# A hybrid decoder layer on one core: the gate products of its linear attention as one float32r pass, and its decays computed within the state space part

## The chip, the core and the metric

One NeuronCore of a Trainium2 chip runs the whole layer as one program. The metric is the device time of one execution in microseconds (us), smaller is better; times given are medians over several executions.

## What is computed

One layer over 512 tokens of width 1024, everything in float32. Cut to what matters here:

```python
h = rms_norm(x, mixer_norm)
q, k, v, g_out, a_lr, z, xbc, dt_raw, gate_a, gate_b = split_cols(h @ w_in, ...)
# linear attention: 4 heads, key width 128 a head, value width 256 a head, chunks of 64
g_log = log_sigmoid(a_lr @ w_gate + b_gate) / 16     # a_lr: 512 x 16, w_gate: 16 x 512
b     = cumsum(g_log within each chunk)
q_t   = q * 128**-0.5 * exp(b);  k_t = k * exp(-b)
o     = causal(q_t k_t^T) v + q_t S_prev             # and k * exp(b_last - b) builds the next state
o_a   = rms(o) * head_norm * silu(g_out)
o_b   = ssd_mixer(z, xbc, dt_raw, ...)               # state space part, 4 groups, chunks of 128
x     = x + (sigmoid(gate_a) * (o_a @ w_branch_a) + sigmoid(gate_b) * (o_b @ w_branch_b)) @ w_out
...                                                  # conv-gated MLP, gated embedding, final norm
```

The change concerns `a_lr @ w_gate` and what is made of it up to `b`.

## The kernel before, in words

**Products.** A float32 product is nearly everywhere made of three float32r passes: each operand is split into a float32r part (`whi`, `h1h`: a cast on ScalarE, L161) and the rest (`wlo`, `h1l`: a subtraction on VectorE, L162), and TensorE multiplies high by high, high by low and low by high into one PSUM tile (`mm3`, L165 to L168). `proj_a` (L170) computes output columns on the partitions, one PSUM tile `pa` of 128x512 for each 128 columns, 24 passes when the inner width is 1024. `proj_b` (L221) computes tokens on the partitions, four PSUM tiles `pb` at once. Both take their tiles from four PSUM banks (tag `mm`, L79); the cores, the transposes and the gate products share four others (tag `sm`, L82). A bank is free again when the function `emit` of the projection has read it.

**Order of the work.** First the norm and its transposes; then the step-size stage (L671 to L734), in which one projection `psdt` of 48 columns gives `dt_raw` and `a_lr`; then the state space part (L736 to L753), for each group `g` a projection (`ssd_proj`), a preparation (`ssd_pre`), the core (`ssd_core`, L584), the gate projection (`ssd_z`), the branch product of the group before (`ssd_branch`) and the gating (`ssd_gate`); then the linear attention (L757 to L927): decays, and for each pair of heads three projections (`gla_pair_proj`, L793: v, then q and k, then g) and two cores (`gla_core`, L846); then the merge (L930 to L968): four pairs of sigmoid gates (`gate_pair`) and four pairs of branch columns (`branch_pair`); then w_out, the MLP and the rest. The order on each engine is not written by hand: a planner takes the instructions that are ready by priority. The priority falls with the place in the program; weight loads and splits are lifted by 100000 (`ahead`, L133), `emit` by 50000, the step-size chain by 60000, and the last `ssd_branch` is put back by 1200 (L750). The order is then fixed, and each engine works through its own queue in it, the DMA queues of SyncE (SP) and ScalarE (ACT) among them.

**The gate products and the decays before.** `alr` (16x512, on partitions 32 to 47) and `wgt` are float32; `wgt` is loaded by one DMA right after the parameters (L492), `alr` is copied out of `psdt` by ScalarE (L677). After the state space part, L770 to L785 compute for each of the four heads: the product `gg` of 16 rows (L772) in float32, an addition, a minimum and an absolute value on VectorE (L776 to L778), Exp on ScalarE (L779), Ln (L783), a subtraction (L784) and a scan (L785) into `bcum`. `gla_pair_proj` makes three exponentials E1, E2, E3 of each `bcum` (L802 to L805), with which `emit` multiplies the projections of q and k (L813, L817, L818).

**Memory.** Pools are laid on a stack in the order in which they are opened, on the left or on the right side, and a closed pool's bytes are given to the next one. A tile of a later pool waits for the older tiles that lay in its bytes. The linear attention lies on the left as `oap` (`oah`, `oal`: 32 KB on each partition), `bcp` (four tiles of 2 KB, tag `bc`: the `bcum`, later gate outputs), then `gp` (`gsm` 2 KB, `v` 16, E1, E2, E3 4 each, `sg` 8, `att`, `qi`, `ks`, `kst` 2 each, `on` 4, `gS` 2, in this order). When `gp` is closed (L926), `mtp` (`mth`, `mtl` 16 KB each, four gate outputs of 2 KB) takes its place. `gate_pair` (L935) writes its sigmoids into `bcp` for columns 0, 1, 4, 5 and into `mtp` for 2, 3, 6, 7 (L938). On the right lies `dts` (L488), closed at L927; the residual tiles `x2` (L972) take its place and are loaded from ScalarE's queue (L974).

Of the kernel before, what the change touches and what calls it, by code (L numbers as in the profile page):

```python
# [8 lines left out]
F32 = mybir.dt.float32  # L9
# [29 lines left out]
def f32(ap):  # L39
    return ap.bitcast(F32)  # L40
# [3 lines left out]
def tile_hybrid_block(  # L44
# [120 lines left out]
    def mm3(ps, lh, ll, rh, rl, first, last):  # L165
        TE.matmul(ps, lhsT=lh, rhs=rh, start=first, stop=False)  # L166
        TE.matmul(ps, lhsT=lh, rhs=rl, start=False, stop=False)  # L167
        TE.matmul(ps, lhsT=ll, rhs=rh, start=False, stop=last)  # L168
# [318 lines left out]
    dx = ExitStack()  # L487
    dts = dx.enter_context(tc.tile_pool(name="dts", bufs=1, side="right"))  # L488

    alr = dts.tile([48, T], F32, name="alr")  # L490
    wgt = dts.tile([48, 512], F32, name="wgt")
    nc.sync.dma_start(wgt[32:48, :], w_gla_gate)  # L492
    qt = dts.tile([P, NT, P], F32, name="qt")

    dram = ctx.enter_context(tc.tile_pool(name="dram", bufs=1, space=bass.MemoryType.DRAM))
# [175 lines left out]
    if True:  # L671
        raw = wload([w_in[:, OFF_DT : OFF_DT + 32], w_in[:, OFF_ALR : OFF_ALR + 16]], KD, 48)
        dhi, dlo = wsplit(raw, KD, 48)
        ps = mm_ps("psdt")
        for k in range(KD):
            mm3(ps[:48, :], dhi[:, k, :], dlo[:, k, :], hT[0][:, k, :], hT[1][:, k, :], k == 0, k == KD - 1)
        S.copy(alr[32:48, :], ps[32:48, :])  # L677
        go = ahead(60000)
        go.__enter__()

        def tl(tag, name, rows=32):
            return sp.tile([rows, T], F32, tag=tag, name=name, bufs=2)

        xr, ab = tl("xdt", "dt_x"), tl("xdt", "dt_ab")
        s1, s2 = tl("xdc", "dt_s1"), tl("xdc", "dt_s2")
        qq, Q = tl("yt", "dt_q"), tl("yt", "dt_Q", P)
        smask = tl("S", "smask")
        G.memset(smask, 1.0)
        G.memset(smask.rearrange("p (c l) -> p c l", c=NT)[:, :, 0:1], 0.0)
        ae = cp.tile([32, 1], F32, name="ae")  # L690
        S.activation(ae, alog, AF.Exp)
        V.tensor_scalar(out=xr, in0=ps[:32, :], scalar1=dtb, scalar2=None, op0=ALU.add)
        V.scalar_tensor_tensor(out=ab, in0=xr, scalar=-1.0, in1=xr, op0=ALU.mult, op1=ALU.max)
        S.activation(ab, ab, AF.Exp, scale=-1.0)

        V.tensor_scalar(out=s1, in0=ab, scalar1=2.0, scalar2=None, op0=ALU.add)
        V.reciprocal(s1, s1)
        V.tensor_tensor(s1, ab, s1, op=ALU.mult)
        V.tensor_tensor(s2, s1, s1, op=ALU.mult)
        V.tensor_scalar(out=qq, in0=s2, scalar1=1.0 / 15.0, scalar2=None, op0=ALU.mult)  # L700
        for k in range(6, 0, -1):
            V.scalar_tensor_tensor(
                out=qq, in0=qq, scalar=1.0 / (2 * k + 1), in1=s2, op0=ALU.add, op1=ALU.mult
            )
        V.scalar_tensor_tensor(out=qq, in0=qq, scalar=1.0, in1=s1, op0=ALU.add, op1=ALU.mult)
        V.tensor_scalar(out=xr, in0=xr, scalar1=0.0, scalar2=None, op0=ALU.max)
        V.scalar_tensor_tensor(out=xr, in0=qq, scalar=2.0, in1=xr, op0=ALU.mult, op1=ALU.add)
        S.copy(Q[0:32, :], xr)

        V.tensor_scalar(out=s1, in0=xr, scalar1=ae, scalar2=None, op0=ALU.mult)  # L710
        V.tensor_tensor_scan(out=s2, data0=smask, data1=s1, initial=0.0, op0=ALU.mult, op1=ALU.add)
        S.copy(Q[32:64, :], s2)
        for c in range(NT):
            nc.scalar.dma_start(ncsd[c], s2[:, c * P : (c + 1) * P])
        S.activation(Q[64:96, :], s2, AF.Exp, scale=-1.0)
        s2v = s2.rearrange("p (c l) -> p c l", c=NT)
        V.tensor_tensor(
            s1.rearrange("p (c l) -> p c l", c=NT), s2v, s2v[:, :, P - 1 : P].to_broadcast([32, NT, P]),
            op=ALU.subtract,
        )  # L720
        S.activation(s1, s1, AF.Exp)
        V.tensor_tensor(qq, s1, xr, op=ALU.mult)
        S.copy(Q[96:128, :], qq)
        ps = sm_ps("psq")
        for c in range(NT):
            TE.transpose(ps[:, c * P : (c + 1) * P], Q[:, c * P : (c + 1) * P], ident)
        V.tensor_copy(qt, ps.rearrange("p (c q) -> p c q", c=NT))
        ps = sm_ps("pscd")
        TE.matmul(
            ps[:, : NT * 32], lhsT=ident[:, P - 1 : P].to_broadcast([P, P]), rhs=qt[:, :, 64:96],  # L730
            start=True, stop=True,
        )
        V.tensor_copy(cdb, ps[:, : NT * 32].rearrange("p (c h) -> p c h", c=NT))
        go.__exit__()  # L734

    ssd_pre(0)  # L736
    ssd_proj(0, 4, 6)
    for g in range(SG):
        ssd_core(g)
        ssd_z(g)  # L740
        if g > 0:
            ssd_branch(g - 1)
        if g + 1 < SG:
            ssd_tiles(g + 1)
            ssd_proj(g + 1, 0, 4)
        ssd_gate(g)
        if g + 1 < SG:
            ssd_pre(g + 1)
            ssd_proj(g + 1, 4, 6)
# [8 lines left out]
    oap = gx.enter_context(tc.tile_pool(name="oap", bufs=1, reuse_waits="tile"))  # L758
    oah = oap.tile([P, KD, T], R, name="oah")
    oal = oap.tile([P, KD, T], R, name="oal")  # L760
    bcp = gx.enter_context(tc.tile_pool(name="bcp", bufs=1, reuse_waits="tile"))
    ggx = ExitStack()
    gp = ggx.enter_context(tc.tile_pool(name="gp", bufs=1, reuse_waits="tile"))
    gsm = gp.tile([P, T], F32, name="gsm")
    G.memset(gsm, 1.0)
    G.memset(gsm.rearrange("p (c l) -> p c l", c=8)[:, :, 0:1], 0.0)
    bcum = [bcp.tile([P, T], F32, tag="bc", name=f"bcum{h}", bufs=4) for h in range(GH)]
    v0 = gp.tile([P, NT, 512], F32, tag="v", name="v0", bufs=2)
    gtmp = []
    for h in range(GH):  # L770
        ps = sm_ps(f"gg{h}")
        TE.matmul(ps, lhsT=wgt[32:48, h * P : (h + 1) * P], rhs=alr[32:48, :], start=True, stop=True)  # L772
        bc = bcum[h]
        e = gp.tile([P, T], F32, tag=f"E{1 + h // 2}", name=f"ge{h}", bufs=2)
        bcol = bga[:, h : h + 1]
        V.tensor_scalar(out=e, in0=ps, scalar1=bcol, scalar2=None, op0=ALU.add)  # L776
        V.tensor_scalar(out=bc, in0=e, scalar1=0.0, scalar2=None, op0=ALU.min)
        V.scalar_tensor_tensor(out=e, in0=e, scalar=-1.0, in1=e, op0=ALU.mult, op1=ALU.max)  # L778
        S.activation(e, e, AF.Exp, scale=-1.0)  # L779
        gtmp.append(e)  # L780
    for h in range(GH):
        bc, e = bcum[h], gtmp[h]
        S.activation(e, e, AF.Ln, bias=1.0)  # L783
        V.tensor_tensor(e, bc, e, op=ALU.subtract)  # L784
        V.tensor_tensor_scan(out=bc, data0=gsm, data1=e, initial=0.0, op0=ALU.mult, op1=ALU.add)  # L785

    def c64(ap):
        return ap.rearrange("p (c l) -> p c l", c=8)
# [139 lines left out]


    mtp = gx.enter_context(tc.tile_pool(name="mtp", bufs=1, reuse_waits="tile"))  # L930
    mth = mtp.tile([P, KD, T], R, name="mth")
    mtl = mtp.tile([P, KD, T], R, name="mtl")
    gates = {}
# [272 lines left out]
```

## Time and profile before

| | us |
|---|---|
| median of 3 runs | 1167.65 |
| lowest and highest | 1167.58, 1169.05 |
| the profiled execution, its time | 1167.36 |
| its span in the profile | 1165.3 |
| TensorE busy in the span | 1143.2 |

The profiled execution is one run of the program; its span goes from the first to the last instruction, and some 2 us of its time lie around it. Engines are named PE (TensorE), PEld (its weight loads), DVE (VectorE), ACT (ScalarE), POOL (GpSimd), SP (SyncE); a name with a q (SPq, ACTq) is the engine's own queue, where DMAs are issued. "L772" is a line of the kernel, `gg<-alr,wgt` an output and its inputs by the program's names. A wait is put down to the instruction whose end released it. Tokens such as "x8" count instructions.

### The profile page before, as it was taken

To read this page: it belongs to the slowest core of one execution; us is meant where nothing else is said; L and a number is where in the kernel's file an instruction comes from. 1 tells how busy PE (TensorE), PEld (TensorE's weight loads), DVE (VectorE), ACT (ScalarE), POOL (GpSimd) and SP (SyncE) were. 2 spreads that over 40 slices of the span, in tenths; PEclk is the share of its full clock that TensorE was granted. 3 is DMA by queue.
4 is the path that set the end of the run, shared out by engine and by line. 5 is a ranking of instruction groups with operands and counts; after the bars stand their busy time and mean duration, and the time that the engine had idled before them with its cause. 6 is when DMAs were issued, how large, how long until landed. Compare 5 with 4: busy or idle time off the path is not lost.

```text
span 1165.3 us, 13943 instructions
## 1 busy us (share of the span) xinstructions
PE 1143.2 (98%) x5476; PEld 947.1 (81%) x5476; DVE 698.4 (60%) x914; ACT 529.8 (45%) x850; POOL 143.4 (12%) x127
## 2 busy tenths in 40 slices
PE   6999999999999999999999999999999999999997
PEld 5888887888888777888888888898888888888786
DVE  6779687866676446343234334555665765776865
ACT  4567756755532147442433232353433433444653
POOL 4003130040041000000021110000030001201112
PEclk9999999999999999999999999999999999999999
DMA  7362443325222423224223431933517552544221
GB/s 211 109 171 70 124 113 104 109 73 145 73 73 73 145 73 109 73 73 109 73 73 91 109 100 46 244 100 109 131 50 181 143 147 73 127 136 109 92 89 73
DMA packets 152673, 125.85 MB, mean 108 GB/s; under 512 B 5776, under 2 KB 125328, under 8 KB 152608
## 3 DMA queue, kind: packets, MB, share of 16 engines
q1 hardware_dynamic: 148352, 115.98, 34.4%
q0 software_dynamic: 2912, 5.77, 2.9%
q10 hardware_dynamic: 1344, 3.21, 0.8%
q8 instruction: 43, 0.70, 0.3%
q14 instruction: 22, 0.18, 0.0%
HBM read 122.79 MB, written 2.16 MB: 107 GB/s over the span
## 4 chain that ended last, share of the span: by engine, by line
PE 92%; DVE 2%; ACT 2%; DMA 1%; SPq 1%; issue 1%; POOL 0%; POOLq 0%; ACTq 0%; DVEq 0%
PE pa L167 17%; PE pa L168 17%; PE pa L166 17%; PE pb L246 7%; PE pb L248 7%; PE pb L247 7%; PE yd L600 2%; PE sX L345 2%; PE sX L346 2%; PE sX L347 2%; DMA raw<-in_w_in_dram 1%; PE st L608 1%; PE yo L597 1%; PE sZ L347 1%; PE sZ L345 1%; PE sZ L346 1%
## 5 line engine op out<-in xcount | busy, mean ns | idle before, releaser
L162 DVE TENSOR_TENSOR wlo<-raw,whi 128x1024 fp32r<-128x1024 f32 (+1 forms) x208 | 259.7, 1256 | 200.7 <-ACT whi L161 200.4
L161 ACT CAST whi<-raw 128x1024 fp32r<-128x1024 f32 (+1 forms) x209 | 215.3, 1033 | 344.0 <-PE pa L167 230.3
L166 PE MATMUL pa<-h1h,whi 128*128 128x512 f32 (+1 forms) x416 | 158.8, 382 | 0.4 <-ACT h1h L416 0.4
L167 PE MATMUL pa<-h1l,whi 128*128 128x512 f32 (+1 forms) x416 | 157.7, 379 | 0.1
L168 PE MATMUL pa<-h1h,wlo 128*128 128x512 f32 (+1 forms) x416 | 157.1, 378 | 0.0
L167 PE MATMUL pa<-h2l,whi 128*128 128x512 f32 (+1 forms) x384 | 142.5, 372 | 0.0
L166 PE MATMUL pa<-h2h,whi 128*128 128x512 f32 (+1 forms) x384 | 142.3, 372 | 0.0
L168 PE MATMUL pa<-h2h,wlo 128*128 128x512 f32 (+1 forms) x384 | 142.0, 372 | 0.0
L246 PE MATMUL pb<-whi,h1h 128*128 128x512 f32 x256 | 100.1, 396 | 2.2 <-DVE accb L660 0.8
L247 PE MATMUL pb<-wlo,h1h 128*128 128x512 f32 x256 | 100.8, 394 | 0.0
L248 PE MATMUL pb<-whi,h1l 128*128 128x512 f32 x256 | 100.0, 393 | 0.0
L167 PEld LDWEIGHTS pa<-h1l,whi 128*128 128x128 f32 x416 | 79.2, 190 | 14.9 <-issue 1.0
L166 PEld LDWEIGHTS pa<-h1h,whi 128*128 128x128 f32 x416 | 79.3, 191 | 14.4 <-ACT h1h L416 0.8
L168 PEld LDWEIGHTS pa<-h1h,wlo 128*128 128x128 f32 x416 | 79.1, 190 | 14.3 <-issue 0.7
L168 PEld LDWEIGHTS pa<-h2h,wlo 128*128 128x128 f32 x384 | 72.3, 188 | 12.6
L167 PEld LDWEIGHTS pa<-h2l,whi 128*128 128x128 f32 x384 | 72.3, 188 | 12.4
L166 PEld LDWEIGHTS pa<-h2h,whi 128*128 128x128 f32 x384 | 72.1, 188 | 12.3
L246 PEld LDWEIGHTS pb<-whi,h1h 128*128 128x128 f32 x256 | 48.1, 188 | 13.6 <-DVE accb L660 1.2
L248 PEld LDWEIGHTS pb<-whi,h1l 128*128 128x128 f32 x256 | 48.1, 188 | 10.6 <-issue 0.7
L247 PEld LDWEIGHTS pb<-wlo,h1h 128*128 128x128 f32 x256 | 48.1, 188 | 10.6 <-issue 0.7
L528 DVE SCALAR_TENSOR_TENSOR acc<-pa,prm,acc 128x511 f32<-128x511 f32 (+2 forms) x72 | 52.7, 743 | 3.2 <-ACT acc L526 2.2
L167 PE MATMUL pa<-obl,whi 128*128 128x512 f32 x128 | 51.2, 400 | 0.0
(365 smaller groups left out, 1970.9 us busy)
## 6 DMA issues: line engine op xcount, KB each, us to landing
raw<-in_w_in_dram SPq DMA_DIRECT2D x48, 512.0 KB, 5.2
raw<-in_w_ffn_up_dram SPq DMA_DIRECT2D x44, 512.0 KB, 5.3
raw<-in_w_in_dram SPq DMA_DIRECT2D x16, 1024.0 KB, 5.1
raw<-in_w_ffn_down_dram SPq DMA_DIRECT2D x10, 1024.0 KB, 5.2
L<-ncsd SPq DMA_DIRECT2D x16, 512.0 KB, 4.6
raw<-in_w_branch_b_dram SPq DMA_DIRECT2D x32, 256.0 KB, 4.0
raw<-in_w_branch_a_dram SPq DMA_DIRECT2D x8, 512.0 KB, 4.6
raw<-in_w_out_dram SPq DMA_DIRECT2D x4, 1024.0 KB, 5.3
```

Source lines behind the costliest of these rows:

```text
L161: S.copy(hi, raw)
L162: eng.tensor_tensor(lo, raw, f32(hi), op=ALU.subtract)
L166: TE.matmul(ps, lhsT=lh, rhs=rh, start=first, stop=False)
L167: TE.matmul(ps, lhsT=lh, rhs=rl, start=False, stop=False)
L168: TE.matmul(ps, lhsT=ll, rhs=rh, start=False, stop=last)
L246: TE.matmul(pss[t], lhsT=a, rhs=hi[:, kk, :], start=first, stop=False)
L247: TE.matmul(pss[t], lhsT=a, rhs=lo[:, kk, :], start=False, stop=False)
L248: TE.matmul(pss[t], lhsT=b, rhs=hi[:, kk, :], start=False, stop=last)
L345: TE.matmul(ps, lhsT=a_h, rhs=hi[:, k % 2, :], start=new and k == 0, stop=False, skip_group_check=True)
L346: TE.matmul(ps, lhsT=a_h, rhs=lo[:, k % 2, :], start=False, stop=False, skip_group_check=True)
L347: TE.matmul(ps, lhsT=a_l, rhs=hi[:, k % 2, :], start=False, stop=k == kh - 1, skip_group_check=True)
L528: V.scalar_tensor_tensor(out=acc[:, s:], in0=ps[:, : T - s], scalar=cw[:, ct, 3 - s : 4 - s], in1=acc[:, s:], op0=ALU.mult, op1=ALU.add,)
```

## The change

`alr` and `wgt` become float32r tiles of 96 partitions. Rows 32 to 47 of `alr` hold the high part of a_lr, rows 0 to 15 its rest, rows 64 to 79 the high part again, all other rows zero; `wgt` holds the high part of the weights in rows 0 to 15 and 32 to 47 and their rest in rows 64 to 79. One pass over 96 rows then adds low by high, high by high and high by low. The weights come by three DMAs into a scratch tile of tag `L`, after GpSimd has zeroed it. The decays are computed in the state space part, after the core of its group 1, with scratch tiles of the tags `xdc`, `xdt` and `yt`; `bcum` moves into `dts`. `bcp` holds gate outputs only, and is opened after `mtp`.

```diff
-    alr = dts.tile([48, T], F32, name="alr")
-    wgt = dts.tile([48, 512], F32, name="wgt")
-    nc.sync.dma_start(wgt[32:48, :], w_gla_gate)
+    alr = dts.tile([96, T], R, name="alr")
+    wgt = dts.tile([96, 512], R, name="wgt")
+    bcum = [dts.tile([P, T], F32, name=f"bcum{h}") for h in range(GH)]
     qt = dts.tile([P, NT, P], F32, name="qt")
...
             mm3(ps[:48, :], dhi[:, k, :], dlo[:, k, :], hT[0][:, k, :], hT[1][:, k, :], k == 0, k == KD - 1)
+        wraw = sp.tile([96, 512], F32, tag="L", name="wraw", bufs=4)
+        G.memset(wraw, 0.0)
+        G.tensor_copy(alr, wraw)
+        for r in (0, 32, 64):
+            nc.sync.dma_start(wraw[r : r + 16, :], w_gla_gate)
+        S.copy(wgt, wraw)
+        V.tensor_tensor(wgt[64:80, :], wraw[64:80, :], f32(wgt[64:80, :]), op=ALU.subtract)
         S.copy(alr[32:48, :], ps[32:48, :])
+        V.tensor_tensor(alr[0:16, :], ps[32:48, :], f32(alr[32:48, :]), op=ALU.subtract)
+        S.copy(alr[64:80, :], alr[32:48, :])
         go = ahead(60000)
...
+    def gla_decays():
+        gsm = sp.tile([P, T], F32, tag="xdc", name="gsm", bufs=2)
+        G.memset(gsm, 1.0)
+        G.memset(gsm.rearrange("p (c l) -> p c l", c=8)[:, :, 0:1], 0.0)
+        gtmp = []
+        for h in range(GH):
+            ps = sm_ps(f"gg{h}")
+            TE.matmul(ps, lhsT=wgt[:, h * P : (h + 1) * P], rhs=alr, start=True, stop=True)
+            bc = bcum[h]
+            e = sp.tile([P, T], F32, tag="xdt" if h < 2 else "yt", name=f"ge{h}", bufs=2)
...
     for g in range(SG):
         ssd_core(g)
+        if g == 1:
+            gla_decays()
         ssd_z(g)
...
-    bcp = gx.enter_context(tc.tile_pool(name="bcp", bufs=1, reuse_waits="tile"))
     ggx = ExitStack()
     gp = ggx.enter_context(tc.tile_pool(name="gp", bufs=1, reuse_waits="tile"))
-    gsm = gp.tile([P, T], F32, name="gsm")
...
-    bcum = [bcp.tile([P, T], F32, tag="bc", name=f"bcum{h}", bufs=4) for h in range(GH)]
     v0 = gp.tile([P, NT, 512], F32, tag="v", name="v0", bufs=2)
...
     mtp = gx.enter_context(tc.tile_pool(name="mtp", bufs=1, reuse_waits="tile"))
+    bcp = gx.enter_context(tc.tile_pool(name="bcp", bufs=1, reuse_waits="tile"))
```

The rest of `gla_decays` is the removed L775 to L785, word for word.

## Rows read from the trace of the kernel before

**Rows 1.** The page: each engine's busy time, share of the span, instructions.
```profile
PE 1143.2 (98%) x5476; PEld 947.1 (81%) x5476; DVE 698.4 (60%) x914; ACT 529.8 (45%) x850; POOL 143.4 (12%) x127
```

**Rows 2.** Stretches: length, then PE, PEld, DVE, ACT, POOL busy, clock, DMA share, GB/s.
```profile
45.00:60.00 15.00, 15.00 (x71) 11.65 (x70) 14.08 (x17) 7.98 (x11) 0.00 (x0) 1.00 0.40 120
...
100.00:160.00 60.00, 60.00 (x309) 49.38 (x309) 48.09 (x59) 42.56 (x80) 13.11 (x11) 1.00 0.39 116
160.00:375.00 215.00, 215.00 (x1056) 176.15 (x1055) 153.16 (x182) 105.21 (x188) 44.38 (x35) 1.00 0.32 95
...
420.00:457.00 37.00, 35.55 (x155) 28.67 (x155) 27.02 (x40) 30.30 (x37) 0.00 (x0) 1.00 0.31 92
457.00:612.00 155.00, 155.00 (x734) 128.01 (x733) 55.06 (x79) 59.22 (x107) 11.46 (x18) 1.00 0.32 87
```

**Rows 3.** Waits of TensorE: waiter, releaser, us in total, times, longest.
```profile
PE pb L246 <- DVE accb L660: 0.8, 1, 0.8
PE pb L246 <- DVE E L818: 0.8, 1, 0.8
PE pb L246 <- DVE E L813: 0.7, 1, 0.7
```

**Rows 4.** Timeline of TensorE around one gate product: start, duration, engine, line.
```profile
382.61 0.39 PE L167 MATMUL pa<-obl,whi 128*128 128x512 f32 x1
...
384.42 0.39 PE L166 MATMUL pa<-obh,whi 128*128 128x512 f32 x1
384.74 1.12 PE L772 MATMUL gg<-alr,wgt 16*128 16x512 f32 x2
385.79 0.50 PE L167 MATMUL pa<-obl,whi 128*128 128x512 f32 x1
386.12 0.40 PE L168 MATMUL pa<-obh,wlo 128*128 128x512 f32 x1
```

**Rows 5.** Instructions on `ge` alone, 419 to 457 us: length, DVE busy, ACT busy.
```profile
419.00:457.00 38.00, 14.21 (x20) 5.06 (x8) 1.00 0.30 90
```

**Rows 6.** ScalarE's groups, 380 to 460 us: busy, mean ns, idle before.
```profile
L783 ACT ACT_TABLE_LOAD x4 | 5.1, 1283 | 0.1
```

**Rows 7.** Step-size stage: instructions on `dt_Q` (ns, start), SyncE's load of `wgt`.
```profile
L726 PE MATMUL psq<-ident,dt_Q x4: 270/272/272, 81.4 to 81.7; 128*128 128x128 f32 x4
...
L723 ACT COPY dt_Q<-dt_q x1: 618/618/618, 78.2 to 78.2; 32x512 f32<-32x512 f32 x1
...
14.38 0.43 SPq L492 DMA_DIRECT2D wgt<-in_w_gla_gate_dram  x1
```

**Rows 8.** ScalarE's queue: two of the four loads of `x2`.
```profile
390.01 0.82 ACTq L974 DMA_DIRECT2D x<-in_x_dram  x2
```

**Rows 9.** Instructions on `pa` alone, by stretch: TensorE's passes first.
```profile
556.60:587.00 30.40, 21.29 (x87) 16.10 (x87) 0.00 (x0) 1.77 (x3) 1.00 0.27 70
...
556.60:611.00 54.40, 41.48 (x170) 31.63 (x170) 0.00 (x0) 2.37 (x4) 1.00 0.31 78
```

**Rows 10.** Timeline of ScalarE: the first and the fifth to seventh gate sigmoid.
```profile
567.62 0.60 ACT L940 ACTIVATE sgt<-pa 128x512 f32<-128x512 f32 x1
...
612.13 1.57 ACT L940 ACTIVATE sgt<-pa 128x512 f32<-128x512 f32 x3
```

**Rows 11.** Timelines of TensorE and VectorE: steps of the core of head 3.
```profile
586.52 0.66 PE L874 MATMUL kst<-ident,ks 128*128 128x128 f32 x4
...
598.10 0.59 PE L891 MATMUL u<-v,kstok 128*128 128x256 f32 x2
598.53 0.59 PE L888 MATMUL o<-gS,qi 128*128 128x256 f32 x2
...
604.21 0.59 PE L888 MATMUL o<-gS,qi 128*128 128x256 f32 x2
...
598.75 0.47 DVE L896 SCALAR_TENSOR_TENSOR gS<-gS,d,u 128x256 f32<-128x256 f32 x1
...
606.91 0.88 DVE L905 SCALAR_TENSOR_TENSOR on<-o,ors,sg 128x256 f32<-128x256 f32 x2 [0.87 <-POOL ors L354]
```

More of the change, by code (lines that the diff above doesn't have):

```diff
@@ L734, in tile_hybrid_block @@
         go.__exit__()
+    def gla_decays():
[8 more added lines that the diff above has]
+            e = sp.tile([P, T], F32, tag="xdt" if h < 2 else "yt", name=f"ge{h}", bufs=2)
+            bcol = bga[:, h : h + 1]
+            V.tensor_scalar(out=e, in0=ps, scalar1=bcol, scalar2=None, op0=ALU.add)
+            V.tensor_scalar(out=bc, in0=e, scalar1=0.0, scalar2=None, op0=ALU.min)
+            V.scalar_tensor_tensor(out=e, in0=e, scalar=-1.0, in1=e, op0=ALU.mult, op1=ALU.max)
+            S.activation(e, e, AF.Exp, scale=-1.0)
+            gtmp.append(e)
+        for h in range(GH):
+            bc, e = bcum[h], gtmp[h]
+            S.activation(e, e, AF.Ln, bias=1.0)
+            V.tensor_tensor(e, bc, e, op=ALU.subtract)
+            V.tensor_tensor_scan(out=bc, data0=gsm, data1=e, initial=0.0, op0=ALU.mult, op1=ALU.add)
     ssd_pre(0)
@@ L760, in tile_hybrid_block @@
     oal = oap.tile([P, KD, T], R, name="oal")
-    bcp = gx.enter_context(tc.tile_pool(name="bcp", bufs=1, reuse_waits="tile"))
     ggx = ExitStack()
     gp = ggx.enter_context(tc.tile_pool(name="gp", bufs=1, reuse_waits="tile"))
-    gsm = gp.tile([P, T], F32, name="gsm")
-    G.memset(gsm, 1.0)
-    G.memset(gsm.rearrange("p (c l) -> p c l", c=8)[:, :, 0:1], 0.0)
-    bcum = [bcp.tile([P, T], F32, tag="bc", name=f"bcum{h}", bufs=4) for h in range(GH)]
     v0 = gp.tile([P, NT, 512], F32, tag="v", name="v0", bufs=2)
[L769 to L785, printed above, removed]
     def c64(ap):
```

## The prediction, made before the changed kernel was built or run

> **What bounds the kernel.** I read the engines' totals first: TensorE is busy for 1143.2 us of a span of 1165.3 [rows 1], so a change pays in two ways only, by TensorE work that goes or by TensorE waits that go. Next, the busy time by stretch [rows 2]: over the state space part (100 to 375 us) and the heads' stretch (457 to 612) TensorE is busy for every microsecond, with VectorE at 80% of its time (48.09 of 60) in one stretch and 71% (153.16 of 215) in the other. What VectorE or ScalarE does there costs nothing as long as TensorE has other ready products. In 420 to 457 us TensorE loses 1.45 us. The list of its waits says to what [rows 3]: 0.8 and 0.7 us for a PSUM bank that VectorE frees by multiplying q or k with E1 to E3, and, just before, 0.8 us for the sum into `accb`. Last, the timeline around a gate product [rows 4].
>
> **Part 1, the gate products: -4.1 us.** Float32r passes start every 0.226 us: eight intervals from 382.61 to 384.42 [rows 4]. Around the gate product, two such passes and the product take 386.12 - 384.42 = 1.70 us. Less 2 x 0.226, one product holds TensorE for 1.25 us, though its two instructions are listed with 1.12 together: the passes beside it are late too. Four make 5.0 us. Afterwards each is one float32r pass; I take the pitch of the neighbours, 4 x 0.226 = 0.9. Gain 4.1 us, with TensorE the bound at either place, so all of it on the path. Ends: 3.8 if the new passes cost 0.3 each beside products of another kind (the pass after the gate product took 0.33), 4.5 if a wait near the first product goes too. The Trainium skill, page "TensorE: Matmul & The Clock Gate", section "Back-to-back issue gap", gives a stream of weight load and matmul some 131 ns a matmul at 512 columns; by that figure the four passes would cost 0.5 and the gain be an estimated 4.5. The 0.226 of the row decides.
>
> **Part 2, the decays leave the start of the linear attention: -1.5 us.** On `ge` alone they cost VectorE 14.21 us and ScalarE 5.06 [rows 5]; the alternation of Exp and Ln costs table loads of 1.28 us, four of them under the Ln line alone [rows 6]. They are why VectorE and ScalarE are at 27.02 and 30.30 of 37 us [rows 2]. Without them E1 to E3 are ready long before q and k come, and the two waits of 0.8 and 0.7 us [rows 3] go. In 457 to 612 us, where the second pair of heads runs the same code without decays, TensorE waits for nothing [rows 2]. The wait of 0.8 for `accb` I leave in: the last branch tile still has to be added before its bank is free. Ends: 0 to 2.3 us.
>
> **Part 3, the decays arrive in the state space part: 0.** VectorE goes from 153.16 to 167.4 us of 215, 78%, below the 80% at which TensorE lost nothing in 100 to 160 us [rows 2]. ScalarE gets 5.06 us and perhaps eight table loads, from 105 to 121 of 215. The products hold up to four `sm` banks and the scratch tiles occupy `xdt`, `yt` and `xdc`, which the cores of groups 1 and 2 use, so a core may finish some microseconds later. The cover is `ssd_z`, the branch product and the next projection, with 96 passes each, 21.7 us each. Were the cover gone, the price would be the waits themselves, 1 to 3 us. Ends: 0 to 3.
>
> **Part 4, the step-size stage: 0.** Added are two VectorE subtractions and two ScalarE copies on the bank `psdt`, at most 0.7 us each (the 32x512 copy in this stage takes 0.62) [rows 7], two GpSimd instructions in a stretch where it does nothing (0.00 of 15 us) [rows 2], and three DMA issues instead of one, at 0.43 each [rows 7]. The DMAs wait for GpSimd and stand in SyncE's queue before weight loads, so a late GpSimd would hold those back; I show no row for the slack of these loads and bound this by the three issues, 1.3 us. The chain that leads to `psq` has 81.4 - 78.8 = 2.6 us to spare [rows 7] against 1.4 on either engine. The old load at 14.38 us goes from the start; TensorE is not fed by it. Ends: 0 to 1.3.
>
> **Part 5, memory that moves: +1.6 us.** Two tiles lie elsewhere. `bcum` in `dts` lives until the exponentials of head 3, so the loads of `x2`, at 390 us before [rows 8], come only then, with 0.4 us each on ScalarE's queue; they are needed after the merge, over 100 us later: 0. But `bcp` now lies above `mtp`, so at bytes 72 to 80 KB of the linear attention's stack (32 + 40, and 8 long). There `gp`, which begins at 32 KB, has the end of `qi` (to 72.1), `ks`, `kst` (to 76.1) and `on` (to 80.1). The first four gate sigmoids must wait until head 3 has done with these; before they lay over `bcum` and ran from 567.62 us on [rows 10]. That such tiles wait shows before as well: `mtp`'s own gate tiles lay over `sg`, and the fifth to seventh sigmoid came in one go at 612.13 [rows 10], with 170 gate passes run by 611 [rows 9], enough for seven tiles of 24.
> Now only four gate tiles fit into PSUM, 96 passes; 87 are used before the core of head 3 reaches its `kst` transposes at 586.52 [rows 9, 11]. The other nine fill 2.0 us, to 589.0. From there the core runs unfilled. Its links: a product 0.43 us (598.10 to 598.53), product `u` to the new state 1.1 (598.10 to 599.2), the last `o` to the scaled rows 3.6 (604.21 to 607.8) [rows 11]. Seven `o` and three `u` fill 4.3 us with some 0.3 idle, to 593.3; `kst` is dead at 592.0, `qi` at 593.3, `on` after its transposes at 596.9. A bank is free one table load (1.28) and one sigmoid (0.6) [rows 6, 10] after such a death: 594.0, 595.2 or 598.8. TensorE idles 1.2, 2.2 or, when only `on` decides, 5.4 us. Two of the four tiles touch `kst` or `qi` without `on`; I take the middle of the first two ways, rounded down: 1.6. Ends: 0 (the planner spreads the passes thinner) and 5.4.
>
> **The sum.** -4.1 - 1.5 + 1.6 = -4.0 us. The profiled execution took 1167.36, so 1163.4; the median of the runs is 0.3 higher, and carried over to it the forecast is 1163.7. A difference of 0.2%, 2.3 us, is about what a measurement of this kernel can tell from no change.
>
> **Rivals.**
> (a) The gate tiles free no bank until `on` is dead: 5.4 instead of 1.6, a sum of -0.2, 1167.5: the same. For it: two of the four tiles do lie over `on`, and the planner sets their order. Against: the two others don't.
> (b) Slower: the 96 passes are gone before the core of head 2 begins, so that two cores run unfilled. Head 2 then idles from the copy of `kst` on, 1.0 + 3.5 (7.8 us of chain to the transposes less 4.3 of products), head 3 1.0 + 5.4: 11 us, a sum of -5.6 + 11 = +5.4, 1173. It decides from 7.9 us of idle time on (5.6 + 2.3). Against: the projections of the second pair of heads come first in priority, and before they fill all of TensorE until head 2's core [rows 2].
> (c) The decays don't get out of the way as hoped: the planner puts them late, or the crowding of part 3 costs TensorE 2 us. Sum -2, 1165.6, on the edge of the measurable. For it: VectorE at 78%, and four `sm` banks at once; against: 80% was free [rows 2].
> (d) The product is not one pass after all. The sum would be +0.1. The new tiles are float32r like `h1h` and `whi`, whose passes took 0.226; I give it no chance of its own.
>
> **Chances.** The forecast 0.60, (a) 0.15, (b) 0.08, (c) 0.17. Faster by over 0.2% (below 1165.3): nearly all of the forecast and somewhat under half of (c), 0.65. The same: (a), the rest of (c), a little of the forecast, 0.25. Slower: (b) and a little, 0.10. Low end of the range: all small waits gone and no starvation, -4.5 - 2.3 = -6.8, 1160.8. High end: (a) with a little of (c), 1168.0. Left out are (b) and the far tails, some 0.13.
>
> **What would show it.** Gate products with one instruction of about 0.39 us each near 160 to 210 us, and none near 385; no table loads of Ln after 375; no waits of TensorE for L813 and L818's successors; TensorE busy for about 1139 us; sigmoids of columns 0 and 1 no earlier than the end of head 3's `u` products, with a TensorE gap of one to two microseconds there. The prediction is wrong if that gap is above 4 us, if the first four sigmoids run as early as before (then 1162), or if TensorE waits in 100 to 375 us.

## The result, and the profile after

The changed kernel takes 1177.21 us (median of 4 runs, 1175.52 to 1177.55) beside 1167.62 for the kernel before on the same chip: ratio 1.0072, 95% interval 1.0061 to 1.0084. It is slower by some 9.6 us, where a gain of 4.0 had been forecast. The profiled execution took 1177.55 us, its span is 1175.8, 10.5 us longer than before.

The page of the changed kernel, its engines line (answers to [rows 1]):

```profile
PE 1145.2 (97%) x5472; PEld 950.7 (81%) x5472; DVE 701.6 (60%) x916; ACT 525.0 (45%) x847; POOL 145.1 (12%) x129
```

TensorE runs four instructions fewer and is yet busy 2.0 us longer. The span grew by 10.5, so it also idles 8.5 us more. Both need an explanation. The list of TensorE's waits names the idle time (waiter, releaser, us in total, times, longest; answers to [rows 3]):

```profile
PE pa L166 <- ACT sgt L954: 2.6, 1, 2.6
PE pb L246 <- DVE acc L529: 2.5, 1, 2.5
PE pa L166 <- DVE acc L529: 2.0, 1, 2.0
PE oaT L925 <- DVE on L918: 1.7, 1, 1.7
PE xn3T L414 <- DVE xn L403: 1.5, 1, 1.5
...
PE o L899 <- ACT on L914: 0.6, 1, 0.6
```

The two waits for the banks that the E tiles free are gone, as forecast. New are two for the convolution sums (`acc`, L529), in the state space part, and three in the core of head 3 (`on`, `sgt`, `on`). The wait for `xn`, at the start, stood at 1.2 before. The busy time by stretch (length, then PE, PEld, DVE, ACT, POOL busy, granted clock, DMA share, GB/s; answers to [rows 2]) adds the other half:

```profile
160.00:375.00 215.00, 210.58 (x1029) 171.66 (x1026) 161.61 (x191) 112.02 (x197) 45.12 (x33) 0.99 0.31 93
205.00:235.00 30.00, 25.58 (x105) 20.43 (x104) 26.61 (x38) 25.79 (x37) 2.64 (x2) 0.94 0.23 71
420.00:457.00 37.00, 36.22 (x160) 29.69 (x159) 16.19 (x23) 16.42 (x22) 0.00 (x0) 1.00 0.37 114
457.00:612.00 155.00, 150.09 (x700) 122.99 (x699) 52.94 (x77) 58.26 (x106) 9.80 (x18) 0.98 0.31 89
560.00:615.00 55.00, 50.09 (x233) 40.46 (x232) 17.60 (x26) 18.89 (x41) 6.08 (x10) 0.94 0.23 58
```

Where TensorE lost nothing before, it now idles 4.42 us (215 less 210.58) and 4.91 us (155 less 150.09), and the clock is below 1.00 exactly in those stretches. Note how small the places are: nearly all of the 4.42 lies in 30 us, where VectorE is busy for 26.61 and ScalarE for 25.79. Over the whole 215 us VectorE is at 75% and ScalarE at 52%.

Where the time went is read from the first instruction of certain tiles on TensorE, taken from the timelines of both kernels. Every later table uses the same five intervals:

| us, before and after | before | after | difference |
|---|---|---|---|
| start to the first `yd` | 104.81 | 106.69 | +1.88 |
| first `yd` to the last `ot` (state space part) | 272.95 | 280.47 | +7.52 |
| last `ot` to the first `att` of head 0 | 97.27 | 90.34 | -6.93 |
| `att` of head 0 to `att` of head 2 | 81.63 | 81.63 | 0.00 |
| `att` of head 2 to `x2n0T` (core of head 3, merge) | 184.28 | 192.03 | +7.75 |

The sum is +10.2, and what follows costs the same (374.83 and 374.82 us up to `x3n2T`). Each row is now read in its timeline.

**The gate products** are one pass each, as forecast (the instructions of the tile `gg`: ns, first and last start):

```profile
L754 PE MATMUL gg<-alr,wgt x4: 393/395/477, 198.8 to 204.8; 96*128 96x512 f32 x4
```

Rows 64 to 79 of such a pass give the third product, the high part of a_lr by the rest of the weights.

**The state space part.** ScalarE's timeline of the changed kernel (start, duration, engine, line, operation; in brackets the idle time before and its releaser):

```profile
210.56 1.28 ACT L761 ACT_TABLE_LOAD   x1
211.85 0.63 ACT L761 ACTIVATE ge<-ge 128x512 f32<-128x512 f32 x1
...
214.12 1.28 ACT L765 ACT_TABLE_LOAD   x1
215.41 0.63 ACT L765 ACTIVATE ge<-ge 128x512 f32<-128x512 f32 x1
216.06 1.28 ACT L761 ACT_TABLE_LOAD   x1
217.36 1.16 ACT L761 ACTIVATE ge<-ge 128x512 f32<-128x512 f32 x2
218.53 1.28 ACT L765 ACT_TABLE_LOAD   x1
219.83 1.15 ACT L765 ACTIVATE ge<-ge 128x512 f32<-128x512 f32 x2
```

Exp (L761) and Ln (L765) alternate, and each change loads a table for 1.28 us: two more loads of the pair follow at 221.93 and 223.88. VectorE takes its instructions in order, and it stands behind these logarithms (VectorE's timeline, then TensorE's, of the same stretch):

```profile
220.49 1.29 DVE L766 TENSOR_TENSOR ge<-bcum,ge 128x512 f32<-128x512 f32 x2 [1.78 <-ACT ge L765]
221.70 0.74 DVE L529 SCALAR_TENSOR_TENSOR acc<-pa,prm,acc 128x509 f32<-128x509 f32 x1
```

```profile
222.59 0.47 PE L166 MATMUL pa<-h1h,whi 128*128 128x512 f32 x1 [1.96 <-DVE acc L529]
...
230.75 0.47 PE L246 MATMUL pb<-whi,h1h 128*128 128x512 f32 x1 [2.46 <-DVE acc L529]
```

VectorE waits 1.78 us for the second and third logarithm, does two subtractions, and only then the convolution sum that frees the PSUM bank on which TensorE waits. The second wait, at 230.75, comes in part the same way: after a subtraction and a scan VectorE idles 0.52 us, until 228.72, for a weight cast that ScalarE makes at 227.65, behind the last two loads of the pair and one more at 225.82. The busy share does not show this, an in-order queue does.

**The core of head 3.** ScalarE, then TensorE:

```profile
600.10 0.69 ACT L927 ACTIVATE oah<-oaT,prm 128x512 fp32r<-128x512 f32 x1 [2.39 <-PE oaT L925]
600.81 1.28 ACT L954 ACT_TABLE_LOAD   x1
602.10 2.07 ACT L954 ACTIVATE sgt<-pa 128x512 f32<-128x512 f32 x4
```

```profile
596.07 0.70 PE L899 MATMUL o<-v,attT 128*128 128x256 f32 x2 [0.62 <-ACT on L914]
...
599.34 0.83 PE L925 MATMUL oaT<-ident,on 128*128 128x128 f32 x4 [1.71 <-DVE on L918]
602.75 0.79 PE L166 MATMUL pa<-h1h,whi 128*128 128x512 f32 x1 [2.58 <-ACT sgt L954]
603.34 0.63 PE L167 MATMUL pa<-h1l,whi 128*128 128x512 f32 x1
603.77 0.63 PE L168 MATMUL pa<-h1h,wlo 128*128 128x512 f32 x1
```

All four sigmoids come in one go at 602.10, after the transposes of `on`; before, the first ran at 567.62 [rows 10]. All 96 gate passes that four banks hold had run by 591.82, and the core then ran with nothing to fill it: 0.62, 1.71 and 2.58 us idle, 4.91 together. When passes begin again at 602.75, they start every 0.43 us instead of 0.226 (603.34 to 603.77). That is the lower of the clock's two levels, 1.2 GHz, and it lasts until 607.18. The windows show the level of a stretch as granted clock (same columns as above):

```profile
232.00:234.00 2.00, 2.00 (x6) 1.52 (x6) 2.00 (x3) 0.00 (x0) 0.00 (x0) 0.50 0.00 0
...
604.00:608.00 4.00, 4.00 (x12) 3.08 (x12) 0.75 (x1) 0.74 (x2) 2.27 (x2) 0.60 0.00 0
```

So TensorE's idle time was paid for again in passes at half speed, and these count as busy: this is why its busy time rose. The same fall follows the wait at 230.75 (0.50 in 232 to 234 us) and the wait for `xn` at the start (0.72 in 22 to 28 us).

### The profile page after: what moved, and what is told of

Read it like the earlier page. It is cut to its first block, busy times and chain, and to the rows that moved or that the text cites. A ratio compares the mean times of both kernels' runs of the same rounds, so it can differ in the third digit from the quotient of the medians.

```text
span 1175.8 us, 13936 instructions
## 1 busy us (share of the span) xinstructions
PE 1145.2 (97%) x5472; PEld 950.7 (81%) x5472; DVE 701.6 (60%) x916; ACT 525.0 (45%) x847; POOL 145.1 (12%) x129
## 4 chain that ended last, share of the span: by engine, by line
PE 93%; ACT 2%; DVE 2%; DMA 1%; SPq 1%; issue 0%; POOL 0%; POOLq 0%; ACTq 0%; DVEq 0%
PE pa L167 18%; PE pa L168 17%; PE pa L166 17%; PE pb L246 8%; PE pb L247 7%; PE pb L248 7%; PE yd L601 2%; PE sX L346 2%; PE sX L345 2%; PE sX L347 2%; PE st L609 1%; PE yo L598 1%; PE sZ L346 1%; PE sZ L345 1%; PE sZ L347 1%; DMA raw<-in_w_in_dram 1%
## 5 line engine op out<-in xcount | busy, mean ns | idle before, releaser
L529 DVE SCALAR_TENSOR_TENSOR acc<-pa,prm,acc 128x511 f32<-128x511 f32 (+2 forms) x72 | 52.6, 743 | 9.4 <-ACT acc L527 8.6
```

The source lines that it names most:

```text
L529: V.scalar_tensor_tensor(out=acc[:, s:], in0=ps[:, : T - s], scalar=cw[:, ct, 3 - s : 4 - s], in1=acc[:, s:], op0=ALU.mult, op1=ALU.add,)
```

## The experiments

Four theories, one for each row of the table that matters, with a rival where there was one. Core of head 3: the place of `bcp` holds the gate tiles back; the rival is that the decays' new place disturbs the order there. State space part: ScalarE's table loads and what queues behind them on VectorE; the rival is VectorE's work itself. Start: the clearing of `alr` on GpSimd. Before the first `att`: one pass for each gate product is worth what was forecast, wherever it runs. The profiled executions give, in the five intervals and in us against the kernel before (the last column goes on to `x3n2T`, and so differs from the sum of the five by up to 0.12):

| kernel | start | state space | to `att` | heads 0, 1 | from head 2 | up to `x3n2T` |
|---|---|---|---|---|---|---|
| the changed kernel | +1.88 | +7.52 | -6.93 | 0.00 | +7.75 | +10.2 |
| e1_bcp_below | +0.35 | +5.93 | -6.94 | +0.01 | 0.00 | -0.7 |
| e2_decays_g3 | +0.35 | +0.96 | -0.41 | 0.00 | +7.75 | +8.6 |
| e3_cast_on_act | +0.09 | +5.95 | -6.94 | +0.01 | +7.99 | +7.0 |
| e4_all_three | -0.03 | +0.97 | +0.37 | 0.00 | 0.00 | +1.3 |
| e5_gates_only | +0.08 | 0.00 | -3.82 | 0.00 | 0.00 | -3.8 |
| e6_no_tables | +0.34 | +3.55 | -6.93 | 0.00 | 0.00 | -3.0 |
| e7_less_dve | +0.34 | +4.54 | -6.94 | +0.01 | 0.00 | -2.1 |
| e8_grouped | +0.45 | +1.25 | -6.95 | -0.03 | -0.04 | -5.4 |
| e9_grouped_cast | -0.15 | +1.28 | -6.94 | -0.03 | -0.04 | -6.0 |
| e10_grouped_old_place | +0.08 | 0.00 | -5.97 | -0.02 | -0.07 | -6.0 |
| e11_above_alone | +0.11 | +0.01 | -3.93 | 0.00 | +8.42 | +4.6 |

In the state space column the four gate passes themselves are 0.96 (e2 and e4, whose gate products start at 365.5 us in e2's trace, inside this interval, while half of the logarithms and all scans fall behind it).

**e1_bcp_below**: the changed kernel with `bcp` opened where it was.

```diff
+    bcp = gx.enter_context(tc.tile_pool(name="bcp", bufs=1, reuse_waits="tile"))
     ggx = ExitStack()
...
     mtp = gx.enter_context(tc.tile_pool(name="mtp", bufs=1, reuse_waits="tile"))
-    bcp = gx.enter_context(tc.tile_pool(name="bcp", bufs=1, reuse_waits="tile"))
```

> The changed kernel with one part undone: the pool of the gate outputs is opened before the linear attention's scratch pool again, as before, so that the first four gate tiles lie over nothing that the cores use; bcum stays where the change put it. Theory (the gate tiles wait for head 3's last tile, TensorE runs out of passes and then runs at the lower clock): the first sigmoid comes before head 3's core again, the waits of 2.6, 1.7 and 0.6 us near 595 to 603 us are gone, and so is the lower clock there; TensorE reached the core of head 2 2.5 us late and the first transpose of the second norm 10.2 us late, so 7.7 us go: 1177.2 - 7.7 = 1169.5. Rival (the cores are late because of the x2 loads on ScalarE's queue or the moved bcum): waits and time stay, 1177.

Measured 1166.83 us, ratio 0.9996 (0.9986 to 1.0005). The last interval is back to that of before, 7.75 us less, and no wait of head 3's core is left: the place of one pool explains that whole row. The time is some 2.6 us lower still (1177.21 less 7.75 is 1169.46). In this profile the clock stayed at 1.00 in 20 to 30 us and in 200 to 240, though the two waits for `acc` are there with 2.0 and 2.5 us as before. The lower clock after such waits therefore comes in some executions and not in others.

**e2_decays_g3**: the decays two groups later. **e4_all_three**: e1, e2 and e3 together.

```diff
-        if g == 1:
+        if g == 3:
             gla_decays()
```

> The changed kernel with the decays computed after the core of group 3 instead of group 1, same scratch tiles; all else as changed. Theory (between 205 and 232 us VectorE and ScalarE are needed for the conv sums of the next projection, the decays stand between, PSUM banks stay full and TensorE waits 2.0 and 2.5 us and then runs at the lower clock): both waits and the clock's drop go, 4.4 + 1.9 = 6.3 us: 1177.2 - 6.3 = 1170.9, if the place after group 3, with VectorE at a third of its time, holds nothing up. Rival (the waits near 220 and 230 us come from the new order of the queues there, not from the decays' work): they stay, 1177.

> The changed kernel with all three edits: gate pool below, decays after the core of group 3, zeroing cast on ScalarE. Theory: the three losses are apart in time and add, 7.7 + 6.3 + 1.9 = 15.9 us: 1161.3, and faster than the kernel before by what the one-pass products and the E1 to E3 waits give, 4.1 + 1.5 = 5.6, that is 1162.0. Rival (the losses have one common cause, or the late decays only move the stall to the start of the linear attention): 1165 or more.

Measured 1176.31 us (ratio 1.0072, 1.0057 to 1.0087) and 1168.63 (1.0002, 0.9992 to 1.0011): both a miss of 5 to 7 us. The state space part did come free, but the crowd moved along. Two waits of e2:

```profile
PE pa L167 <- DVE obl L650: 2.2, 1, 2.2
PE pa L166 <- ACT obh L649: 2.1, 1, 2.1
```

Now the last branch product waits for its operands `obh` and `obl`, which ScalarE and VectorE make after the decays' work: in e2 the `obh` (382.38) follow a load and a logarithm (380.56, 381.85), the `obl` (386.00) two scans (383.15, 384.87). The granted clock fell as well (0.50 in 384 to 390 us of e2, 0.50 in 386 to 390 of e4), and of the -6.93 at the start of the linear attention -0.41 is left. What the decays cost is not a matter of group 1: at the other place, too, they stood in two in-order queues ahead of something that TensorE needed, and cost it over 4 us of waits and the slow passes behind them.

**e3_cast_on_act**: `alr` is cleared by ScalarE.

```diff
-        G.tensor_copy(alr, wraw)
+        S.copy(alr, wraw)
```

> The changed kernel with one instruction on another engine: the cast that zeroes alr runs on ScalarE instead of GpSimd; the order on TensorE and VectorE is the same. Theory (GpSimd's cast of 1.33 us at 21.6 us holds up VectorE's two scalings of xn, 1.22 us instead of 0.87, TensorE's gap at 22 us gets 0.3 us longer and the lower clock follows until 27 us): the two scalings take 0.87 again, no lower clock in the start, 1.9 us less: 1175.3. Rival (the lower clock in the start comes and goes with the execution): the scalings may be shorter but the time moves by 0.3 at most, 1176.9.

Measured 1175.2 us, ratio 1.0064 (1.0047 to 1.0082). The wait for `xn` is 1.2 us again, and the first `yd` comes 0.26 us earlier than in e1 and e2, which kept the cast on GpSimd and had no lower clock at the start either. So the collision costs about 0.3 us; the other 1.5 of the changed kernel's +1.88 is clock, which stood at 0.83 in 20 to 30 us of its profile and at 1.00 in those of e1 and e2, whose code is the same up to there.

**e5_gates_only**: the kernel before with the 96-row float32r tiles and nothing else, cleared by ScalarE.

```diff
-    alr = dts.tile([48, T], F32, name="alr")
-    wgt = dts.tile([48, 512], F32, name="wgt")
-    nc.sync.dma_start(wgt[32:48, :], w_gla_gate)
+    alr = dts.tile([96, T], R, name="alr")
+    wgt = dts.tile([96, 512], R, name="wgt")
...
-        TE.matmul(ps, lhsT=wgt[32:48, h * P : (h + 1) * P], rhs=alr[32:48, :], start=True, stop=True)
+        TE.matmul(ps, lhsT=wgt[:, h * P : (h + 1) * P], rhs=alr, start=True, stop=True)
```

> The kernel before with the one-pass gate products alone: float32r tiles of 96 rows, filled in the step-size stage (the zeroing cast on ScalarE); the decays are computed at the start of the linear attention as before, and all pools lie as before. Theory (the products themselves are worth 4.1 us, 1.25 against 0.23 us each, and nothing else moves): 1167.7 - 4.1 = 1163.6, with four gg passes of about 0.39 us listed and TensorE busy some 4 us less. Rival (the products fill a gap in which TensorE waits for the first obl anyway, so that little is gained, or the new order brings a stall of its own): 1166 to 1168.

Measured 1163.83 us, ratio 0.9955 (0.994 to 0.9969), as expected. All of it lies in one interval, -3.82 us.

**e6_no_tables**: e1 with Identity in place of Exp and Ln; exponential and logarithm are left out, and with them the six table loads of the pair and one more (L536). All other instructions keep their order on every engine.

```diff
-            S.activation(e, e, AF.Exp, scale=-1.0)
+            S.activation(e, e, AF.Identity, scale=0.0)
...
-            S.activation(e, e, AF.Ln, bias=1.0)
+            S.activation(e, e, AF.Identity, scale=1.0)
```

> The run with the pool below (e1_bcp_below) in which the decays' Exp and Ln are replaced by Identity on the same tiles, so that the exponential and the logarithm are left out of the decays; the order on TensorE, VectorE, GpSimd and SyncE is the same, only ScalarE's table loads go. Theory A (the eight table loads of 1.28 us, 10.3 us on ScalarE, which the order does not allow for, make VectorE wait at the subtraction and the conv sums behind it late): the waits of 2.0 and 2.5 us near 220 and 230 us go, 4.5 us less than e1_bcp_below: 1162.3. Theory B (VectorE's 15 us of decay work fill it up): the waits stay within 1 us, 1166.8.

Measured 1164.48 us, ratio 0.9963 (0.9949 to 0.9977), between the two theories. In the state space part the excess over the four passes falls from 4.97 (5.93 less 0.96) to 2.59 us. The wait of 2.0 us shrinks to 0.2; of the other, 1.8 of 2.5 is left:

```profile
PE pb L246 <- DVE acc L529: 1.8, 1, 1.8
```

The loads are half of it. Of the rest VectorE's timeline shows no idle time between 211.97 and the end of that wait (226.83), and scans and a subtraction still stand ahead of the convolution sum:

```profile
220.86 2.33 DVE L767 TENSOR_TENSOR_SCAN bcum<-gsm,ge 128x512 f32<-128x512 f32 x2
223.11 0.67 DVE L766 TENSOR_TENSOR ge<-bcum,ge 128x512 f32<-128x512 f32 x1
223.69 1.22 DVE L767 TENSOR_TENSOR_SCAN bcum<-gsm,ge 128x512 f32<-128x512 f32 x1
...
225.94 1.40 DVE L529 SCALAR_TENSOR_TENSOR acc<-pa,prm,acc 128x509 f32<-128x509 f32 x2
```

**e7_less_dve**: e1 with a simpler decay; the absolute value, the second minimum and the subtraction are left out.

```diff
-            V.tensor_scalar(out=e, in0=ps, scalar1=bcol, scalar2=None, op0=ALU.add)
-            V.tensor_scalar(out=bc, in0=e, scalar1=0.0, scalar2=None, op0=ALU.min)
-            V.scalar_tensor_tensor(out=e, in0=e, scalar=-1.0, in1=e, op0=ALU.mult, op1=ALU.max)
-            S.activation(e, e, AF.Exp, scale=-1.0)
+            V.tensor_scalar(out=e, in0=ps, scalar1=bcol, scalar2=0.0, op0=ALU.add, op1=ALU.min)
+            S.activation(e, e, AF.Exp)
...
-            V.tensor_tensor(e, bc, e, op=ALU.subtract)
```

> The run with the pool below (e1_bcp_below) with half of the decays' work on VectorE left out (minimum, absolute value and subtraction; the decays are then the scan of ln(1+exp(min(x,0)))); Exp and Ln stay, and so do their table loads. Theory A (table loads): VectorE has 7 us less to do there but TensorE still waits 3 us or more between 200 and 240 us: 1165 to 1167. Theory B (VectorE is full): the waits go, 1162.3.

Measured 1166.25 us, ratio 0.9979 (0.9966 to 0.9991). The time lies where the table loads were said to put it, but the run is inconclusive: the order changed with the work. Four loads stand at the pair's lines instead of six, yet the trace has 33 in all, against 32 in e1: others took their place. With less work on VectorE and no fewer loads the excess is still 3.58 us, now as two waits, 3.1 us together and the longest 2.7, for another operand (`xt` for `acc`).

**e8_grouped**: e1, with all four exponentials ahead of all four logarithms. The bias of Ln is a column of ones that is made from the four results of Exp, so no Ln can start before the last Exp.

```diff
+        one = cp.tile([P, 1], F32, name="one")
+        for h in range(GH):
+            V.tensor_scalar(
+                out=one, in0=gtmp[h][:, :1], scalar1=0.0, scalar2=1.0 if h == 0 else one, op0=ALU.mult, op1=ALU.add
+            )
         for h in range(GH):
             bc, e = bcum[h], gtmp[h]
-            S.activation(e, e, AF.Ln, bias=1.0)
+            S.activation(e, e, AF.Ln, bias=one)
```

> The run with the pool below (e1_bcp_below) in which no Ln can start before the last Exp: the bias of the four Ln is a column of ones made from the results of all four Exp, by four small additions on VectorE. Theory A (table loads): two to four table loads of the decays instead of eight, 5 to 8 us less on ScalarE, and the waits near 220 and 230 us shrink below 1 us: 1162 to 1163.5. Theory B: unchanged, 1166.8.

Measured 1161.91 us, ratio 0.9939 (0.9923 to 0.9956): faster than both kernels. Everything is computed, and VectorE has four small instructions more, so VectorE's amount of work was not the bound. TensorE is full again in the stretch where it lost 4.4 us (window of e8_grouped):

```profile
205.00:235.00 30.00, 29.99 (x145) 24.76 (x144) 28.21 (x44) 25.96 (x39) 2.11 (x2) 1.00 0.28 85
```

VectorE is busier (28.21 of 30 us, 94%) than in the changed kernel (26.61) and TensorE loses nothing. The grouping did two things at once: the loads of the pair fell from six to two (L538 has one more), and on VectorE the convolution sums at 216.53 to 223.18 now come ahead of the subtractions (224.09) and scans (226.54). e6 takes away the loads and keeps the order, and 2.59 us of excess stay; e8 changes both, and 0.29 stay (1.25 less 0.96). So the order counts beside the loads. What it is worth alone, with all six loads in place, no run shows.

**e9_grouped_cast**: e8 with the cast on ScalarE (the edit of e3). **e10_grouped_old_place**: e5 with the same `one` column in the old place; the decays are not moved and no memory is. **e11_above_alone**: e5 with `bcum` in `dts` and `bcp` above `mtp`; the decays are not moved.

```diff
+    bcum = [dts.tile([P, T], F32, name=f"bcum{h}") for h in range(GH)]
...
-    bcp = gx.enter_context(tc.tile_pool(name="bcp", bufs=1, reuse_waits="tile"))
...
     mtp = gx.enter_context(tc.tile_pool(name="mtp", bufs=1, reuse_waits="tile"))
+    bcp = gx.enter_context(tc.tile_pool(name="bcp", bufs=1, reuse_waits="tile"))
```

> Grouped logarithms with `bcp` below (as in e8_grouped), and the copy that clears `alr` on ScalarE instead of GpSimd. If the collision at the start of GpSimd's cast with VectorE's scaling costs what the traces of after showed, 0.35 us, the time is about 0.35 us under e8_grouped's ratio: ratio near 0.9936. If it costs more than that in most executions (a lower clock after the gap): 1 to 2 us under e8_grouped, ratio near 0.992. If neither: the same as e8_grouped.

> The kernel before with one-pass gate products and with all exponentials ahead of all logarithms, the decays left where they were, at the start of the linear attention. If the table loads of ScalarE hold E1 to E3 there, the two TensorE waits of 0.7 us that e5_gates_only had for L821 and L826 go, and the time is that of e5_gates_only less 1.4, ratio near 0.994: then moving the decays is not what pays. If VectorE's work alone holds them, the waits stay and the time is that of e5_gates_only, ratio 0.9955.

> The kernel before with one-pass gate products (as e5_gates_only), the running sums in `dts` and `bcp` opened above `mtp` as the change has it, the decays left where they were. If the place of `bcp` alone costs what the core of head 3 lost in the trace of after (7.75 us from head 2 to the merged tile), the time is that of e5_gates_only plus 7.75, ratio near 1.002, with TensorE waits for `sgt` of L954's kind. If the loss needs the moved decays as well, the time is that of e5_gates_only, ratio 0.9955.

e9: 1161.37 us, ratio 0.9936 (0.9923 to 0.9948), 0.5 us under e8's median, with 0.6 of the difference at the start; the interval does not part it from e8. e10: 1161.49 us, ratio 0.9937 (0.9924 to 0.9951), the same as e9. ScalarE's table loads at the start of the linear attention fall to one for L787 and one for L796 (seven in e5), and the waits for the E tiles are gone. Window of e5_gates_only, then of e10_grouped_old_place:

```profile
420.00:457.00 37.00, 35.56 (x155) 28.66 (x154) 25.83 (x38) 28.47 (x36) 0.00 (x0) 1.00 0.38 114
```

```profile
420.00:457.00 37.00, 37.00 (x165) 30.65 (x164) 27.08 (x43) 22.16 (x31) 0.00 (x0) 1.00 0.45 142
```

What the move was to bring, the end of those waits, is to be had without the move. e11: 1172.03 us, ratio 1.0027 (1.0018 to 1.0036), 8.2 us above e5's median. The last interval gives 8.42. Of what that has over 7.75, 0.6 is clock: 13 passes ran at the lower level (596.47 to 602.18) instead of ten. Its waits carry the signature of the changed kernel, without moved decays:

```profile
PE pa L166 <- ACT sgt L948: 2.6, 1, 2.6
PE oaT L919 <- DVE on L912: 1.7, 1, 1.7
```

Together with e1 this settles the core of head 3: the place of `bcp` does it, without the moved decays too, and `bcum` lies in `dts` in e1 and e11 alike. The changed kernel's timeline says what held the two gate tiles that do not touch `on` when it ran. In ScalarE's order all four sigmoids stand behind the `oah` of 600.10, which waited 2.39 us for the transposes of `on`, while the tile of `kst` (`kstok`) had last been read by the `u` product of 594.41 and `qi` by the `o` product of 596.60. Why they were given that place, for the bytes' sake or not, no run shows.

## Why the prediction was wrong

**Part 1 was right.** Forecast -4.1, with ends 3.8 and 4.5; measured -3.82 (e5).

**Part 2 was right in its mechanism, and too small.** Forecast -1.5. Of the -6.93 before the first `att`, 3.82 are the shorter gate products and 0.96 their passes that now run elsewhere; 2.15 are left. I had added up the listed waits, and a listed wait is less than what it costs. TensorE's timeline of e5_gates_only at one of them:

```profile
448.62 0.40 PE L248 MATMUL pb<-whi,h1l 128*128 128x512 f32 x1
449.72 0.50 PE L246 MATMUL pb<-whi,h1h 128*128 128x512 f32 x1 [0.70 <-DVE E L821]
450.06 0.39 PE L247 MATMUL pb<-wlo,h1h 128*128 128x512 f32 x1
```

The list counts from the end of the pass before, which is modelled 0.40 long and would have overlapped the next one. From start to start it is 1.10 instead of 0.226, and the next start is late by another 0.11: 0.98 us for a listed 0.70. The count of passes in the two windows above says the same: ten more in 37 us (165 against 155) are 10 x 0.226 = 2.3 us.

**Part 3 failed**: forecast 0 with an end of 3, measured 6.6 (7.52 less 0.96), of which 4.97 stay in e1, whose clock did not fall there. Rival (c) had 2 us for this crowding. The step that failed is "78%, below the 80% at which TensorE lost nothing". A busy share measured over 215 us says nothing of a burst of 30 us, and a share at which nothing was lost is no threshold: e8 loses nothing at 94%. What decides is what stands ahead of what in each queue. I counted eight table loads as busy time, never as 1.28 us each in front of the logarithms that VectorE's next instruction waits for. The order of e6 is the same with and without these loads, so it seems that the planner did not allow for them. Grouping was worth 2.15 us in the old place (5.97 less 3.82, e10 and e5) and 4.68 in the new one (5.93 less 1.25, e1 and e8), the reordering that came with it included. The Trainium skill, page "ScalarE: Activation LUTs", section "Table sets: the hidden batching unit", says to batch calls by set. e8 and e10 agree, with Exp and Ln loaded here as two sets (last section).

**Part 4 failed in a small way**: forecast 0 with an end of 1.3, measured 1.88. I placed the new GpSimd work in the stretch of the step-size stage, where GpSimd idles. But the clearing of `alr` depends on nothing, and it ran at 21.58 us, beside the scalings that TensorE awaited. The start lost 0.35 by that and the other new work (e1), 0.26 of it by this collision (e1 less e3); the rest is clock.

**Part 5 had the mechanism right and the size wrong**: forecast +1.6, measured +7.75. The step is "I take the middle of the first two ways": I counted on the two tiles that do not touch `on` to go first. The four went together, after `on`. That is rival (a), priced at 5.4 against 4.91 listed as idle; the clock and the late starts after three waits make up the rest. (The first of the two ways, 1.2 us, comes to 1.0 by its own terms, 0.3 and 594.0 less 593.3; that hardly moves the 1.6.) It was given a chance of 0.15 although the row of the old kernel in which three sigmoids come in one go [rows 10] spoke for it.

**What no part had** is the clock. Each idle time was priced as idle time alone. Of the +10.2, about 1.5 at the start, 1.6 in the state space part (7.52 against 5.93 in e1) and 2.2 in the core of head 3 (the ten passes from 602.75 to 607.18 took 4.43 us instead of 2.26) are passes at the lower level: some 5 us. Without them the change would still be slower, by about 5. Rival (b), the slower one, was another mechanism and did not happen: head 2's core kept its passes (in 559.13 to 595.40 us TensorE is busy for all of 36.27). Two signs that the prediction had named for being wrong did come, a gap of over 4 us in head 3's core (4.91) and waits of TensorE in 100 to 375 us (4.42). TensorE was to be busy for 1139 us and was for 1145.2.

The sum as measured: 1.88 + 6.6 - 3.82 - 2.15 + 7.75 = +10.3, against 10.2 in the trace.

## What to carry to other kernels

Before work is moved under a busy TensorE, ask of each in-order queue what will stand behind it and who waits for that; a mean busy share cannot answer this, and a table load between Exp and Ln belongs in that count. Opening a pool at another place in the stack is an edit of its own: list whose bytes it now takes and when these die, and take the latest death as the price unless the order of the waiting engine excludes it. Here the simple half of the change (one pass for each gate product, -3.8 us) plus a grouping of Exp and Ln in the old place (-2.2 us) gives 1161.5 us; with the move, at its best, it was 1161.4.

## What was not expected of the hardware

**A gap can cost twice.** After gaps of TensorE the granted clock fell to 0.50, the 1.2 GHz level, and passes started every 0.43 us instead of 0.226. After the gaps of head 3's core (4.91 us within the 7.3 to 602.75) it did so in all four profiles that have them: the changed kernel, e2 and e3 (0.50 in 600 to 604 us) and e11 (0.50 in 598 to 602). After the shorter waits it did so in some executions only: in the changed kernel after the second (230.75; 0.50 in 232 to 234), in e3 after the first (220.79; 0.51 in 222 to 224), in e1 after neither (1.00 in 200 to 240). In e3 the fall cost nothing in the end: the wait behind it was 0.8 us instead of the 2.5 of e1, and the interval grew by as much (5.95 and 5.93). So there the slow passes only shortened the next wait, as VectorE's sum, and not TensorE, set the pace. That short waits drop the clock in some executions only fits the steps between executions of one kernel: of e1's ten runs six lie at 1166.73 to 1166.86, three at 1168.34 to 1168.43 and one at 1170.02, about 1.6 us apart, the size of one such fall at the start (1.88 less 0.35). The kernel before makes the same steps: of its fifteen runs beside e9 to e11 six lie at 1167.27 to 1167.66 with a mean granted clock of 0.997 or 0.998, seven at 1169.04 to 1169.25 with 0.996 or 0.997, and two at 1170.72 with 0.995. So the steps go with the clock; where it fell in those runs, which have no profile, is not shown. A median of a few runs depends on the steps they fell on (1167.62 in the first comparison, 1169.12 beside e9 to e11), so a ratio may hold about 0.1% of such steps.

**GpSimd slows VectorE.** While GpSimd copied `wraw` to `alr`, two scalings on VectorE took 1.22 us instead of 0.87 (the changed kernel, then the one before):

```profile
21.58 1.33 POOL L680 CAST alr<-wraw 96x512 fp32r<-96x512 f32 x1
```

```profile
22.36 1.22 DVE L403 TENSOR_SCALAR xn<-xn,xn3r 128x512 f32<-128x512 f32 x2
```

```profile
22.39 0.87 DVE L403 TENSOR_SCALAR xn<-xn,xn3r 128x512 f32<-128x512 f32 x2
```

The Trainium skill, page "SBUF — State Buffer", section "Who interferes with whom", says that the two engines share a pair of ports, that scalings can be among what needs it, and that the engine that comes second stands still until the first is done. The trace agrees in kind, not in size: the cast lasted 0.55 us beyond VectorE's start, and VectorE lost 0.35. With the cast on ScalarE (e3) the two scalings took 0.87 again.

**Exp and Ln do not share a table here.** In the timelines read here each change from one to the other comes with a load of 1.28 us. The Trainium skill, page "ScalarE: Activation LUTs", section "Table sets: the hidden batching unit", names a set that holds both functions. No run here shows that set in use.
